# Moving a layer norm's shift and sums to VectorE, holding condition rows behind the norm, and splitting pool bands inside the short convolution

## The chip, the cores and the metric

The kernel runs on one core of a Trainium2 chip. The metric is the device time of one execution in microseconds. In the text PE is TensorE, DVE is VectorE, ACT is ScalarE, POOL is GpSimd and SP is SyncE, whose queue issues the DMAs.

## The reference

One step of a backbone of four layers for 128 context tokens and 256 latent tokens, D = 1024, in float32. Each layer has a mixer and an MLP, each followed by a layer norm of a scaled residual. The mixers are: a gated linear recurrence (layers 0 and 3), a short gated convolution (layer 1), a pooling mixer (layer 2).

```python
for i in range(DEPTH):
    mod = jax.nn.silu(cond) @ p['w_mod'][i] + p['b_mod'][i]
    sh1, sc1, g1, sh2, sc2, g2 = jnp.split(mod[:, None, :], 6, axis=-1)
    h = x * (1 + sc1) + sh1
    ...                                   # out = mixer(h)
    x = layer_norm(ALPHA * x + g1 * out, p['ln_g'][i, 0], p['ln_b'][i, 0])
    h = x * (1 + sc2) + sh2
    f = squared_relu_mlp(h, p['mlp_w1'][i], p['mlp_b1'][i], p['mlp_w2'][i], p['mlp_b2'][i])
    x = layer_norm(ALPHA * x + g2 * f, p['ln_g'][i, 1], p['ln_b'][i, 1])
```

The pooling mixer takes windowed means of 2, 4, 8 and 16 tokens in four groups of channels; the kernel does that as a product with banded matrices.

## The kernel before, in words

**Layout.** Features lie on the 128 partitions, the 384 tokens (128 + 256) along the free axis. The residual stream is eight tiles `X0` to `X7` of 128 x 384, one for each 128 features ("column" c below).

**Products.** A float32 product is done as three matmuls (L198, L199, L200): each weight and each activation is split into a rounded part `hi` and a rest `lo`, and hi x hi, lo x hi and hi x lo are summed in PSUM. One weight tile of 128 x 128 with its three matmuls is called a tile here. Weights come as 1 MB blocks of 16 tiles by DMA (L1275, four buffers `raw`), and a block is split in two halves of 8 tiles: ACT writes `whi` (L1287), DVE writes `wlo` (L1293). The split of a half is asked for three halves ahead of its use.

**Order of work.** The program is a list `items` of blocks in order: `X` (a function), `G` (a function with a loaded block), and halves of weights. Every tile is a tick; `defer(n, fn)` runs `fn` n ticks later. From that the framework makes one fixed queue for each engine: it may move an instruction ahead of earlier ones of the program when its inputs are there. `tc.issue_after(ins)` puts instructions behind `ins` in the queue of its engine, without a semaphore.

**Layer norm.** `ln_evac` runs while the product ahead of the norm is computed. For each finished column c, `resid` (L556, two DVE instructions for the two token groups) adds the gated output to `X[c]`. Once column 0 is there, `shift` takes its mean over the partitions (L578 on PE, L579 on ACT into `ssb`) and subtracts it from all eight columns (L581), which keeps the variance formula well conditioned. `stat` then squares each column (L592, ACT) and adds columns and squares into the running sums `s1t` (L596) and `s2t` (L598). With `fast=True` (the recurrence layers and the pooling layer) the subtractions of columns 3 to 7 and the sums `s2t` are on DVE; the subtractions of columns 0 to 2 and `s1t` are on POOL. With `late=True` (the pooling layer alone) the shift is on DVE already and the squares are summed on PE. In all other norms shift and sums are on POOL.

`ln_tail` follows. `stats_a` sums over the partitions on PE: `s1t` (L620), `s2t` (L622), the last column (L623) and its square (L624). Condition products (`gemv`, L348) fill PE while DVE and ACT do the tail: variance (L652), reciprocal root (L653, ACT), centring (L643), one Newton step (L657 to L659), scaling (L663) and the next `h` (L698, L703, L716, L721, L760). The last instruction of the tail, the `lo` half of `h` of column 7 on DVE, is kept as `hcur["end"]`.

**MLP.** `up` (L819 to L822) makes the hidden tiles `hid`, in `hi` and `lo`; the down projection reads them in order of k, 16 at a time.

**Condition rows.** Some of the modulation vectors are computed on DVE during the MLPs (`mac`, L453): products of weight rows (`fetch`, L445, two buffers in the tile `mac`) with the row `silb`, which is silu of the condition, repeated on all partitions. `silb` is made once, at the start of the first MLP, by `setup_rows`: a tanh (L429, ACT), a scale (L430, DVE) and a product (L431, DVE) over 2048 elements each. It uses the second `mac` buffer as its scratch, so the second `fetch` comes behind it. The products L453 are already held behind `hcur["end"]`.

**Bands.** `band_load(i)`, i = 0 and 1, loads a block of band matrices and splits it (L1091 on ACT, three L1095 on DVE). They are needed by the pooling mixer in layer 2. In the program they stand between the second layer norm and the short convolution of layer 1.

## Time and profile before

| | us |
|---|---|
| median of 3 runs | 1624.18 (1623.5 to 1624.21) |
| the profiled execution | 1623.76 |
| its span | 1621.9 |
| PE busy in it | 1569.9 |
| DVE busy | 1158.7 |
| ACT busy | 750.6 |
| POOL busy | 392.8 |
| granted PE clock, mean | 0.996 |

A row of the profile's timeline gives the start, the duration, the engine, the line of the kernel, the operation, what it writes and reads with the shapes, how many like it were merged, and in brackets the idle time of the engine ahead of it with what ended it. Times are microseconds from the start of the span. Rows of one engine overlap a little, since an instruction may start while the last one drains; the distance from start to start is then shorter than the duration.

### The profile page before, as it was taken

Reading aid. Unit: us, or ns where it says so; the run is one execution under the profiler, and the core shown is the slowest. Engines: PE = TensorE matmul, PEld = TensorE weight load, DVE = VectorE, ACT = ScalarE, POOL = GpSimd, SP = SyncE. Lnnn points to the kernel's source line nnn. Section 1 sums busy time; section 2 is a strip of 40 time slices with the busy share of each in tenths; the row PEclk is TensorE's granted clock in tenths of the full one; section 3 lists DMA queues with packets and bytes.
Section 4 is the critical chain, followed back from the end, with each engine's and each line's share of the span. In section 5 each row is a group of like instructions: output and inputs, shape, how many; then the busy total and the mean of one; then the engine's idle time right before and its main releaser. Section 6 shows DMA issues by size and latency. Waiting matters only on the chain.

```text
span 1621.9 us, 23848 instructions
## 1 busy us (share of the span) xinstructions
PE 1569.9 (97%) x9388; PEld 1500.4 (93%) x9388; DVE 1158.7 (71%) x1786; ACT 750.6 (46%) x1129; POOL 392.8 (24%) x410
## 2 busy tenths in 40 slices
PE   6999899999999999999999999999999989999996
PEld 6778799999989989999998799999988779999996
DVE  4789899974475559994545999974468997434544
ACT  3796553244352336423434653244359947423432
POOL 2113290001430067300043290000431134000043
PEclk9999999999999999999999999999999999999999
DMA  9677457755353345765453357745333444333321
GB/s 361 264 277 275 138 204 256 266 201 208 130 176 115 139 181 194 243 229 181 139 197 131 144 208 255 268 159 197 120 118 104 161 141 154 122 117 125 130 78 39
DMA packets 42591, 289.79 MB, mean 179 GB/s; under 512 B 4848, under 2 KB 7024, under 8 KB 8432
## 3 DMA queue, kind: packets, MB, share of 16 engines
q1 hardware_dynamic: 42480, 288.28, 49.8%
q8 instruction: 73, 1.20, 0.3%
q14 instruction: 38, 0.31, 0.0%
HBM read 286.67 MB, written 1.59 MB: 178 GB/s over the span
## 4 chain that ended last, share of the span: by engine, by line
PE 79%; DVE 12%; ACT 5%; issue 2%; DMA 1%; POOL 1%; SPq 0%; DVEq 0%; POOLq 0%; ACTq 0%
PE acc L199 25%; PE acc L198 25%; PE acc L200 25%; DVE wlo L1293 2%; DVE lru L868 1%; ACT hidf L919 1%; DMA raw<-in_wmod 1%; DVE X L556 1%; DVE hidf L947 1%; DVE hidf L936 1%; ACT L922 1%; ACT hidf L922 1%; DVE X L663 1%; DVE X L581 0%; ACT L932 0%
## 5 line engine op out<-in xcount | busy, mean ns | idle before, releaser
L1287 ACT ACTIVATE whi<-raw 128x1024 fp32r<-128x1024 f32 x338 | 356.1, 1056 | 413.4 <-PE acc L200 345.2
L1293 DVE TENSOR_TENSOR wlo<-raw,whi 128x1024 fp32r<-128x1024 f32 x338 | 435.3, 1289 | 154.9 <-ACT whi L1287 154.4
L198 PE MATMUL acc<-h,whi 128*128 128x384 f32 (+2 forms) x1472 | 499.0, 339 | 7.2 <-DVE h L698 6.7
L199 PE MATMUL acc<-h,wlo 128*128 128x384 f32 (+2 forms) x1472 | 498.3, 339 | 0.0
L200 PE MATMUL acc<-h,whi 128*128 128x384 f32 (+2 forms) x1472 | 468.8, 339 | 0.0
L198 PE MATMUL acc<-hid,whi 128*128 128x384 f32 (+1 forms) x1216 | 411.3, 338 | 0.8 <-ACT hid L964 0.8
L200 PE MATMUL acc<-hid,whi 128*128 128x384 f32 (+1 forms) x1216 | 409.9, 337 | 0.8 <-DVE hid L968 0.8
L199 PE MATMUL acc<-hid,wlo 128*128 128x384 f32 (+1 forms) x1216 | 409.2, 336 | 0.0
L198 PEld LDWEIGHTS acc<-h,whi 128*128 128x128 f32 x1472 | 277.1, 188 | 14.7 <-issue 10.0
L199 PEld LDWEIGHTS acc<-h,wlo 128*128 128x128 f32 x1472 | 277.0, 188 | 1.0 <-issue 0.2
L200 PEld LDWEIGHTS acc<-h,whi 128*128 128x128 f32 x1472 | 273.7, 188 | 1.0 <-DVE X L643 0.4
L198 PEld LDWEIGHTS acc<-hid,whi 128*128 128x128 f32 x1216 | 228.4, 188 | 2.3 <-ACT hid L964 1.4
L200 PEld LDWEIGHTS acc<-hid,whi 128*128 128x128 f32 x1216 | 228.2, 188 | 1.5 <-DVE hid L968 1.5
L199 PEld LDWEIGHTS acc<-hid,wlo 128*128 128x128 f32 x1216 | 228.2, 188 | 0.9
L453 DVE SCALAR_TENSOR_TENSOR mac<-mac,silb 128x1024 f32<-128x1024 f32 x176 | 216.3, 1229 | 1.7
L819 ACT ACTIVATE tmp<-acc,par 128x384 f32<-128x384 f32 x128 | 74.2, 580 | 248.1 <-PE acc L200 248.1
L581 POOL TENSOR_TENSOR X<-X,ssb 128x384 f32<-128x384 f32 x46 | 52.5, 1178 | 488.1 <-ACT ssb L579 488.1
L821 DVE TENSOR_TENSOR tmp<-tmp 128x384 f32<-128x384 f32 x128 | 73.2, 572 | 104.1 <-ACT tmp L819 104.1
L556 DVE SCALAR_TENSOR_TENSOR X<-acc,m,X 128x128 f32<-128x128 f32 (+1 forms) x176 | 64.6, 410 | 109.2 <-PE acc L200 109.2
L771 POOL TENSOR_SCALAR X<-X,ag,xbb 128x128 f32<-128x128 f32 x64 | 134.2, 2112 | 0.4
L822 DVE TENSOR_TENSOR hid<-tmp,hid 128x384 fp32r<-128x384 f32 x128 | 72.2, 564 | 0.3
L596 POOL TENSOR_TENSOR s1t<-s1t,X 128x384 f32<-128x384 f32 x40 | 43.7, 1092 | 114.4 <-DVE X L556 111.1
(192 smaller groups left out, 1192.4 us busy)
## 6 DMA issues: line engine op xcount, KB each, us to landing
raw<-in_w SPq DMA_DIRECT2D x128, 1024.0 KB, 4.9
mac<-in_wmodv SPq DMA_DIRECT2D x44, 1024.0 KB, 5.2
raw<-in_wmodp SPq DMA_DIRECT2D x26, 1024.0 KB, 4.9
park<-in_wmodp SPq DMA_DIRECT2D x18, 1024.0 KB, 8.4
raw<-in_lin SPq DMA_DIRECT2D x16, 1024.0 KB, 4.9
raw<-in_scin SPq DMA_DIRECT2D x12, 1024.0 KB, 4.8
raw<-in_wmod SPq DMA_DIRECT2D x8, 1024.0 KB, 7.7
raw<-in_lout SPq DMA_DIRECT2D x8, 1024.0 KB, 5.0
```

Source lines behind the costliest of these rows:

```text
L198: pe.matmul(ps, lhsT=hi, rhs=xhi, start=first, stop=False)
L199: pe.matmul(ps, lhsT=lo, rhs=xhi, start=False, stop=False)
L200: late = lambda: pe.matmul(ps, lhsT=hi, rhs=xlo, start=False, stop=last)
L453: vec.scalar_tensor_tensor(prod, raw[i % 2][:, D * q : D * q + D], 1.0, silb[:, D * k : D * k + D], op0=ALU.mult, op1=ALU.mult, accum_out= ...
L556: vec.scalar_tensor_tensor(Xt[c][:, o : o + n], ps[:, a:b], col(g, c, k), Xt[c][:, o : o + n], op0=ALU.mult, op1=ALU.add)
L581: (vec if late or fast and i > 2 else gp).tensor_tensor(Xt[i], Xt[i], ssb, op=ALU.subtract)
L771: gp.tensor_scalar(Xt[c][:, a:b], Xt[c][:, a:b], col(g, c, k), col(xb, c, k), op0=ALU.mult, op1=ALU.add)
L819: act.activation(r, ps[:, :T], AF.Relu, bias=par_t[:, i : i + 1])
L821: vec.tensor_tensor(q, r, r, op=ALU.mult)
L822: vec.tensor_tensor(lo, q, hi.bitcast(F32), op=ALU.subtract)
L1287: act.activation(hi, raws[id(raw)][:, i * 1024 : (i + 1) * 1024], AF.Copy)
L1293: vec.tensor_tensor(lo, raws[id(raw)][:, i * 1024 : (i + 1) * 1024], hi.bitcast(F32), op=ALU.subtract)
```

## The change

Three edits. (1) In the norms with `fast=True` and not `late`, which are the first norms of layers 0 and 3, all eight subtractions of the shift and the six additions of `s1t` are issued on DVE. (2) The three instructions of `setup_rows` are issued inside `tc.issue_after(hcur["end"].ins)`. (3) `band_load(0)` and `band_load(1)` are inserted into the short convolution's items, behind its 10th and its 12th half of weights.

```diff
     def setup_rows(t):
         nc.sync.dma_start(silb, crow)
-        defer(6, lambda: act.activation(t, silb, AF.Tanh, scale=0.5))
-        defer(10, lambda: vec.tensor_scalar(t, t, 1.0, 0.5, op0=ALU.add, op1=ALU.mult))
-        defer(14, lambda: vec.tensor_tensor(silb, t, silb, op=ALU.mult))
+
+        def behind(fn):
+            def f():
+                with tc.issue_after(hcur["end"].ins):
+                    fn()
+
+            return f
+
+        defer(6, behind(lambda: act.activation(t, silb, AF.Tanh, scale=0.5)))
+        defer(10, behind(lambda: vec.tensor_scalar(t, t, 1.0, 0.5, op0=ALU.add, op1=ALU.mult)))
+        defer(14, behind(lambda: vec.tensor_tensor(silb, t, silb, op=ALU.mult)))
         rows_ready.append(True)
...
             for i in [0] + held if late else range(C):
-                (vec if late or fast and i > 2 else gp).tensor_tensor(Xt[i], Xt[i], ssb, op=ALU.subtract)
+                (vec if late or fast else gp).tensor_tensor(Xt[i], Xt[i], ssb, op=ALU.subtract)
...
             if 0 < c < 7:
-                gp.tensor_tensor(s1t, Xt[0] if c == 1 else s1t, Xt[c], op=ALU.add)
+                (gp if late else s2eng).tensor_tensor(s1t, Xt[0] if c == 1 else s1t, Xt[c], op=ALU.add)
...
     ln_tail(2, to_h(2, "mm"), use)
-    band_load(0)
-    band_load(1)
+    here = len(items)
     use = short_conv(1)
+    for i in range(2):
+        band_load(i)
+        items.insert(here + 11 + 3 * i, items.pop())
     ln_tail(3, to_h(3, "mm"), use)
```

## The prediction

> **What bounds the kernel now.** I read the page first, then who TensorE (PE) waits for, then each of the three stretches that the diff touches in order of time, engine by engine.

> ```profile
> span 1621.9 us, 23848 instructions
> PE 1569.9 (97%) x9388; PEld 1500.4 (93%) x9388; DVE 1158.7 (71%) x1786; ACT 750.6 (46%) x1129; POOL 392.8 (24%) x410
> ```

> ```profile
> PE acc L620 <- POOL s1t L596: 7.0, 2, 5.1
> ...
> PE acc L198 <- DVE h L698: 6.7, 6, 2.0
> ```

> PE is busy for 1569.9 of 1621.9 us, so only what ends a PE pause can move the end. The second fence lists such pauses (total us, times, longest). The line with POOL's running sum `s1t` stands for exactly two pauses, 5.1 and 1.9 us: the first layer norm of layer 0 ("first site") and of layer 3 ("second site"), where the diff moves work. The third place is the layer norm before the short convolution ("band site"), one of the six pauses before L198.

> First site, rows of PE, DVE, ACT and POOL in order of time (start, us, what, count, idle before):

> ```profile
> 151.85 1.92 ACT L429 ACTIVATE mac<-silb 128x2048 f32<-128x2048 f32 x1 [1.14 <-DVE hid L968]
> 153.68 1.04 ACT L1287 ACTIVATE whi<-raw 128x1024 fp32r<-128x1024 f32 x1
> 153.80 1.23 DVE L430 TENSOR_SCALAR mac<-mac 128x2048 f32<-128x2048 f32 x1 [0.26 <-ACT mac L429]
> ...
> 155.18 4.45 POOL L581 TENSOR_TENSOR X<-X,ssb 128x384 f32<-128x384 f32 x3 [6.41 <-ACT ssb L579]
> 156.08 4.91 DVE L581 TENSOR_TENSOR X<-X,ssb 128x384 f32<-128x384 f32 x5
> ...
> 165.58 2.28 DVE L431 TENSOR_TENSOR silb<-mac,silb 128x2048 f32<-128x2048 f32 x1
> ...
> 169.09 1.28 ACT L602 ACT_TABLE_LOAD   x1
> ...
> 170.00 2.02 DVE L1293 TENSOR_TENSOR wlo<-raw,whi 128x1024 fp32r<-128x1024 f32 x1
> ...
> 173.29 2.26 POOL L596 TENSOR_TENSOR s1t<-s1t,X 128x384 f32<-128x384 f32 x2 [2.35 <-DVE X L556]
> ...
> 175.60 1.65 PE L620 MATMUL acc<-s1t,ones_m 128*128 128x384 f32 x2 [5.11 <-POOL s1t L596]
> 175.89 0.73 DVE L556 SCALAR_TENSOR_TENSOR X<-acc,m,X 128x128 f32<-128x128 f32 x2
> 177.04 1.49 PE L622 MATMUL acc<-s2t,ones_m 128*128 128x384 f32 x2
> ...
> 181.20 0.56 DVE L652 SCALAR_TENSOR_TENSOR tmp<-acc,tmp 128x384 f32<-128x384 f32 x1 [4.58 <-PE acc L624]
> 181.68 1.01 DVE L643 TENSOR_TENSOR X<-X,acc 128x384 f32<-128x384 f32 x2
> 182.60 0.55 DVE L657 TENSOR_TENSOR tmp<-tmp,tmp 128x384 f32<-128x384 f32 x1
> ...
> 183.75 1.90 PE L348 MATMUL acc<-raw,sil 128*32 128x256 f32 x32
> ...
> 185.84 0.41 PE L198 MATMUL acc<-h,whi 128*128 128x384 f32 x1 [0.19 <-DVE h L698]
> ```

> The reader sees three things. PE has finished the mixer's matmuls at 175.60 - 5.11 = 170.49. The last residual (L556 at 175.89) is 5.4 us later than that, because DVE runs behind: L430 and L431, which belong to the next stage, sit in its queue, and its rows are stretched while POOL reads the same tiles: five subtractions take 4.91 beside POOL's three, while two of the same size take 0.92 from start to start (181.68 to 182.60) when POOL is quiet. And the pause also costs afterwards: the two statistics matmuls of L622 last 1.49 here against 0.81 at the second site.

> Second site:

> ```profile
> 1312.76 4.91 DVE L581 TENSOR_TENSOR X<-X,ssb 128x384 f32<-128x384 f32 x5 [0.46 <-ACT ssb L579]
> ...
> 1322.91 1.21 DVE L1293 TENSOR_TENSOR wlo<-raw,whi 128x1024 fp32r<-128x1024 f32 x1
> ...
> 1325.33 2.03 DVE L556 SCALAR_TENSOR_TENSOR X<-acc,m,X 128x128 f32<-128x128 f32 x6
> ...
> 1330.00 0.91 PE L620 MATMUL acc<-s1t,ones_m 128*128 128x384 f32 x2 [1.94 <-POOL s1t L596]
> 1330.29 0.73 DVE L556 SCALAR_TENSOR_TENSOR X<-acc,m,X 128x128 f32<-128x128 f32 x2
> 1330.75 0.81 PE L622 MATMUL acc<-s2t,ones_m 128*128 128x384 f32 x2
> ...
> 1332.96 0.56 DVE L652 SCALAR_TENSOR_TENSOR tmp<-acc,tmp 128x384 f32<-128x384 f32 x1 [1.95 <-PE acc L624]
> ```

> Same picture without the condition rows: PE ends at 1328.06, the last residual at 1330.29 + 0.73 = 1331.0, and `s1t` keeps PE only 1.94 us.

> **The change part by part.**

> *Shifts and sums to DVE.* POOL loses three subtractions and six `s1t` additions at each of the two sites; DVE gets them. Its unstretched step is 0.46 us (above), a pair of residual halves 0.68 (2.03 for six halves), a weight split 1.21. The work between the shift and the last residual is then 8 subtractions + 6 `s1t` + 6 `s2t` = 20 x 0.46 = 9.2, 7 pairs = 4.7, 2 splits = 2.4: 16.3 us in all. At the second site it starts at 1312.76 and ends at 1329.1; PE's own end would allow 1328.06 + 0.1 + 0.7 = 1328.9, so DVE is just about the limit. Gain 1331.0 - 1329.1 = 1.9; the square of the last column and its matmul follow in the same way. I take 1.7, because the ACT table load (1.28) sits in the chain of squares that `s2t` waits for. Bounds: 2.1 (PE's end) and -0.5 (if DVE's steps came to 0.58 each, 20 x 0.12 = 2.4 more).

> *Condition rows behind the first layer norm.* The two DVE instructions L430 and L431 (1.23 + 2.28 = 3.5) leave the first site; ACT's L429 (1.92) ran beside the matmuls and the row after it shows no wait for it, so it may stay or go at no cost here. There the first split can start when its high half is ready, 153.68 + 1.04 = 154.72, ends at 155.9, and the same 16.3 us put the last residual at 172.2 instead of 176.6. PE's floor is 170.49 + 0.8 = 171.3. From there: square 0.5, one statistics pair 0.65 (1330.00 to 1330.75 and on, less its overlap), so L652 starts at about 173.5 instead of 181.20: 7.7 us. Of these 4.4 are the earlier residual, and the rest is that three of the four statistics pairs no longer stand behind the late `s1t` at the slow rate. What follows is unchanged: L652 to the first matmul is 4.64 us (181.20 to 185.84), and PE fills it with the condition matmuls of L348, which end at 185.65. I take 7.3, with 0.4 off for the table load; ends 8.6 (PE's floor) and 3.5 (only the two rows' time comes back).

> *What the moved rows cost later.* They now stand behind the last instruction of the norm, where the next MLP starts:

> ```profile
> 240.00:280.00 40.00, 40.00 (x231) 40.00 (x231) 39.79 (x65) 14.14 (x18) 0.39 (x2) 1.00 0.73 252
> ...
> 253.13 0.34 PE L198 MATMUL acc<-hid,whi 128*128 128x384 f32 x1
> ...
> 257.90 0.56 DVE L822 TENSOR_TENSOR hid<-tmp,hid 128x384 fp32r<-128x384 f32 x1
> ...
> SPq L445 <- DVE silb L431: 11.3, 1, 11.3
> ```

> (The first row is a stretch of the MLP: PE, PE loads, DVE, ACT, POOL busy.) DVE has no room there, 39.79 of 40 us, so 3.5 us stay as a backlog. Behind them on DVE are the weight splits, the hidden-layer halves and the condition products L453, which need the rows. The tightest reader is the down projection: a tile of PE's work is three matmuls, 0.52 us (231 matmuls in 40 us), so its 16th k comes at 253.13 + 15 x 0.52 = 260.9; that low half is ready at 257.90 + 0.56 = 258.5, 2.4 us ahead. A backlog of 3.5 leaves PE 1.1 us short at worst; the low half is used by the third matmul of a tile only (0.35 later), and some of the backlog falls on L453. I take 0.3, ends 0 and 1.1; if the tanh L429 were held back too, with a table load, 1.92 + 1.28 = 3.2 more is the outer end. SP: the second condition load L445 waited 11.3 us for L431 and nothing behind it was late; it now waits for the later L431, with weight loads of the MLP behind it. Each block feeds PE for 16 x 0.52 = 8.3 us, and there are four buffers; I put nothing on it.

> *Band splits into the short convolution.* The band site, then a stretch of the short convolution:

> ```profile
> 454.25 0.59 DVE L1095 TENSOR_TENSOR fine<-raw,band 128x256 fp32r<-128x256 f32 x3 [4.56 <-ACT band L1091]
> ...
> 457.69 0.56 DVE L652 SCALAR_TENSOR_TENSOR tmp<-acc,tmp 128x384 f32<-128x384 f32 x1 [1.87 <-PE acc L624]
> 458.60 1.07 ACT L1091 ACTIVATE band<-raw 128x1040 fp32r<-128x1040 f32 x1 [1.17 <-DMA raw<-in_band]
> 459.58 0.51 ACT L653 ACTIVATE tmp<-tmp 128x384 f32<-128x384 f32 x1
> 460.09 1.91 PE L348 MATMUL acc<-raw,sil 128*32 128x256 f32 x32
> 460.19 0.56 DVE L657 TENSOR_TENSOR tmp<-tmp,tmp 128x384 f32<-128x384 f32 x1 [1.01 <-ACT tmp L653]
> ...
> 463.71 0.41 PE L198 MATMUL acc<-h,whi 128*128 128x384 f32 x1 [1.71 <-DVE h L698]
> ```

> ```profile
> 500.00:515.00 15.00, 15.00 (x88) 15.00 (x87) 8.70 (x16) 4.46 (x6) 0.00 (x0) 1.00 0.42 140
> ```

> ACT's queue stands for the second band's DMA and then splits it (458.60) before the reciprocal root L653, which was ready at 458.25. L652 to the first matmul takes 6.02 here, 4.64 at the first site: 1.4 us too long. PE's condition matmuls end at 462.0, before the new 462.3, so they don't take the gain. The moved work is two ACT splits (1.07 each), six small DVE instructions (0.59 for three) and two DMAs past 10 and 12 half blocks of SP's weight loads. It lands some 42 and 50 us after 463.71 (a half block is 8 tiles, 4.2 us), where DVE has 6 and ACT 10 of 15 us free. The loads keep a lead of three half blocks. Cost 0, gain 1.4; ends 1.7 (the whole pause) and 0.

> *The sum.* 7.3 + 1.7 + 1.4 - 0.3 = 10.1 us. The profiled execution took 1623.76, 0.4 below the median of the runs (1624.18): 1623.76 - 10.1 = 1613.7. The sum with all ends kind is 8.6 + 2.1 + 1.7 = 12.4, which gives 1611.4.

> [...] PE's slow statistics follow a pause of 5.11 us, those after 1.94 are fast; what lies between these two the trace does not show, and 3 pairs x 0.65 = 2.0 us hang on it. [...]

> **The rivals.**

> (a) *DVE becomes the late engine at the first site.* If its queue puts splits or waits for squares ahead of the `s1t` additions, the sums come 3 us or more after PE's end and the slow rate stays. The DVE row of 16.3 us leaves no idle at all, which speaks for it; that the last column's eight tiles (8 x 0.52) give DVE 4.2 us from about 166.3 on, in which PE brings it nothing new, speaks against. Then 2.0 for the slow pairs and 1 of delay are lost: about 1616.7.

> (b) *The backlog stops PE in the MLP.* With L429 held back as well the backlog is 6.7 us, 4.3 beyond the 2.4 of margin, of which 0.3 is in the sum: 1613.7 + 4.0 = 1617.7. ACT's free time speaks against, DVE's full row for it.

> (c) *The rows are not moved:* an order among DVE's instructions alone, or a schedule that keeps L430 in the norm. The first site then gains about 4.2: 1616.8.

> (d) *Slower:* the long DVE rows are DVE's own and not POOL's doing. At 0.93 a step (as in the stretched 4.91 for five) nine more instructions cost 8.4 us at the second site and 8.4 - 3.5 at the first; with -1.4 for the bands about 1634. It decides from a step of roughly 0.75 on; the 0.46 of L643 without POOL speaks strongly against.

> **How the numbers follow.** Forecast, all three parts as summed (1611.4 to 1615.5): 0.70. (a) 0.12, (b) 0.07, (c) 0.05, (d) 0.02, and 0.04 for gains eaten elsewhere, near no change. The time predicted is the first one's, 1613.7. The range reaches from the kind ends, 1611.4, past (a), (b) and (c) to 1618.5. What a measurement here can tell from no change is about 0.2%, 3.2 us; faster by more than that: 0.94, within 0.03, slower 0.03.

> **What will show it.** In the changed profile L581 and L596 at both sites are DVE rows of some 0.5 us each, and POOL is quiet there; the wait of L620 on POOL is gone, with less than 1.5 us in its place; L622 at the first site takes 0.81; L430 and L431 lie after the norm's last `h`; L653 at the band site follows L652 at once and the wait there is about 0.3. The forecast is wrong if L620 waits for DVE for over 3 us, if PE waits for `hid` L822 or a split at the start of the down projection, or if DVE's steps stay near 0.9 without POOL.

## The result, and the profile after

The changed kernel takes 1616.08 us (median of 4 runs, 1615.73 to 1617.12) against 1624.2 (4 runs, 1623.5 to 1625.98): a ratio of 0.9947, 95% interval 0.9935 to 0.996. A later set of more runs gave 1616.25 (5 runs) against 1625.6 (12 runs), 0.9946 (0.9933 to 0.9958). The prediction said 1613.7, between 1611.4 and 1618.5. The profiled execution took 1615.74, 8.02 less than the one before.

In the changed kernel the lines from about L436 on stand 8 lower in the file: L429 to L431 are L437 to L439, L556 is L564, L581 is L589, L596 is L604, L620 to L624 are L628 to L632, L652 is L660, L698 is L706. Behind the moved bands it is 10: L1287 is L1297, L1293 is L1303. In the variants below the numbers shift again; there the names of the tiles say which row it is.

The page's first part and the table of PE's waits, after:

```profile
span 1614.0 us, 23830 instructions
PE 1567.8 (97%) x9388; PEld 1499.6 (93%) x9388; DVE 1155.0 (72%) x1804; ACT 750.7 (47%) x1129; POOL 373.7 (23%) x392
```

```profile
PE acc L198 <- DVE h L706: 5.5, 6, 2.0
...
PE acc L628 <- DVE s1t L604: 2.0, 2, 1.0
```

The two pauses behind `s1t` went from 7.0 us to 2.0, and it is now DVE that ends them. The waits ahead of L198 went from 6.7 to 5.5.

The first site after (rows of ACT, DVE and PE in the timeline; POOL has none between 150 and 190 us):

```profile
152.93 1.92 ACT L437 ACTIVATE mac<-silb 128x2048 f32<-128x2048 f32 x1 [1.14 <-DVE hid L976]
...
155.82 1.23 DVE L1303 TENSOR_TENSOR wlo<-raw,whi 128x1024 fp32r<-128x1024 f32 x1 [1.20 <-ACT whi L1297]
156.97 3.83 DVE L589 TENSOR_TENSOR X<-X,ssb 128x384 f32<-128x384 f32 x8
...
171.87 0.55 DVE L604 TENSOR_TENSOR s1t<-s1t,X 128x384 f32<-128x384 f32 x1
172.34 0.55 DVE L606 TENSOR_TENSOR s2t<-s2t,tmp 128x384 f32<-128x384 f32 x1
172.81 0.48 DVE L564 SCALAR_TENSOR_TENSOR X<-acc,m,X 128x256 f32<-128x256 f32 x1
175.50 0.56 DVE L660 SCALAR_TENSOR_TENSOR tmp<-acc,tmp 128x384 f32<-128x384 f32 x1 [2.22 <-PE acc L632]
...
195.06 1.22 DVE L438 TENSOR_SCALAR mac<-mac 128x2048 f32<-128x2048 f32 x1
```

```profile
172.57 0.88 PE L628 MATMUL acc<-s1t,ones_m 128*128 128x384 f32 x2 [1.00 <-DVE s1t L604]
173.29 0.81 PE L630 MATMUL acc<-s2t,ones_m 128*128 128x384 f32 x2
173.93 0.81 PE L631 MATMUL acc<-X,ones_m 128*128 128x384 f32 x2
174.58 0.81 PE L632 MATMUL acc<-tmp,ones_m 128*128 128x384 f32 x2
...
180.14 0.41 PE L198 MATMUL acc<-h,whi 128*128 128x384 f32 x1 [0.30 <-DVE h L706]
```

Eight subtractions now take 3.83 us, 0.47 each from start to start; five took 4.91 beside POOL. The pause is 1.00 us, the statistics matmuls run at 0.65 a pair, and L438, the first moved row on DVE, stands behind the norm. The tanh on ACT (L437) did not move, although its line is wrapped in the same way: it still runs ahead of the norm, at 152.93 (L429 at 151.85 before). The second site after, and the end of PE's work at the band site:

```profile
1321.15 0.35 DVE L564 SCALAR_TENSOR_TENSOR X<-acc,m,X 128x128 f32<-128x128 f32 x1 [0.35 <-PE acc L200]
1321.41 0.55 DVE L604 TENSOR_TENSOR s1t<-s1t,X 128x384 f32<-128x384 f32 x1
1321.88 0.55 DVE L606 TENSOR_TENSOR s2t<-s2t,tmp 128x384 f32<-128x384 f32 x1
1322.11 0.88 PE L628 MATMUL acc<-s1t,ones_m 128*128 128x384 f32 x2 [1.00 <-DVE s1t L604]
1322.35 0.48 DVE L564 SCALAR_TENSOR_TENSOR X<-acc,m,X 128x256 f32<-128x256 f32 x1
1325.04 0.56 DVE L660 SCALAR_TENSOR_TENSOR tmp<-acc,tmp 128x384 f32<-128x384 f32 x1 [2.22 <-PE acc L632]
```

```profile
451.98 0.56 DVE L660 SCALAR_TENSOR_TENSOR tmp<-acc,tmp 128x384 f32<-128x384 f32 x1 [1.87 <-PE acc L632]
...
456.70 0.41 PE L198 MATMUL acc<-h,whi 128*128 128x384 f32 x1 [0.40 <-DVE h L706]
```

From the variance row to the first matmul the band site now takes 4.72 us, not 6.02. The two band splits on ACT stand at 479.72 and 489.21, 23 and 33 us behind that matmul, and between 457 and 520 us no row of PE shows a wait.

To see where time goes in any variant I cut each trace at two kinds of rows that all of them have, the start of the shift (`ssb`, L579 or its counterpart) and of the variance (L652 or its counterpart), eight norms each. Where nothing was changed, the traces agree to some 0.1 us between these points, so what differs can be put to a place. Three things are outside that: the slow stretches of experiment 4, the band column of the four traces with unmoved bands, which spreads over 0.4 (112.98 to 113.38), and the start, which spreads over 1 us even without a slow stretch. The columns: start of the first shift; first site, shift to variance; second norm's variance to third norm's shift (it holds the band site); fifth variance to sixth shift (unchanged code); second site, shift to variance; start of the last variance row. The variants are explained below.

| trace | start | first site | band | 5th to 6th | second site | last |
|---|---|---|---|---|---|---|
| before | 154.62 | 26.58 | 113.24 | 217.66 | 20.73 | 1609.76 |
| before, second | 155.36 | 26.59 | 112.98 | 217.64 | 20.74 | 1610.32 |
| after | 155.69 | 19.81 | 111.92 | 217.67 | 19.76 | 1601.82 |
| after, second | 156.39 | 19.80 | 111.92 | 217.64 | 19.77 | 1602.53 |
| after, third | 154.93 | 19.80 | 111.92 | 219.20 | 19.77 | 1602.58 |
| sums alone | 154.91 | 19.97 | 113.38 | 217.64 | 19.79 | 1602.71 |
| rows alone | 155.54 | 22.83 | 113.09 | 217.66 | 20.73 | 1606.84 |
| bands alone | 155.11 | 26.59 | 111.91 | 219.17 | 22.24 | 1612.37 |
| column 6 on PE | 155.40 | 19.86 | 111.91 | 219.19 | 19.82 | 1603.19 |
| its square on PE | 155.59 | 19.54 | 111.91 | 219.19 | 19.17 | 1602.36 |
| idle POOL adds | 154.65 | 26.73 | 111.92 | 219.20 | 25.91 | 1615.36 |
| pauses filled | 155.30 | 19.80 | 111.92 | 217.65 | 19.76 | 1601.76 |
| square and two fills | 155.53 | 19.54 | 111.92 | 217.64 | 19.19 | 1600.76 |

Between the first two traces (before and after): 6.77 won at the first site, 1.32 at the band site, 0.97 at the second site, 1.07 lost before the first shift, in code that the change does not touch; 7.94 in all (with 0.05 lost between, by differences of a few hundredths).

### The profile page after: what moved, and what is told of

Same layout as the page of the kernel before. It is cut to its first block, busy times and chain, and to the rows that moved or that the text cites. A ratio compares the mean times of both kernels' runs of the same rounds, so it can differ in the third digit from the quotient of the medians.

```text
span 1614.0 us, 23830 instructions
## 1 busy us (share of the span) xinstructions
PE 1567.8 (97%) x9388; PEld 1499.6 (93%) x9388; DVE 1155.0 (72%) x1804; ACT 750.7 (47%) x1129; POOL 373.7 (23%) x392
## 4 chain that ended last, share of the span: by engine, by line
PE 81%; DVE 11%; ACT 5%; issue 1%; DMA 1%; POOL 0%; SPq 0%; DVEq 0%; POOLq 0%; ACTq 0%
PE acc L199 26%; PE acc L200 26%; PE acc L198 26%; DVE wlo L1303 2%; DVE lru L876 1%; ACT hidf L927 1%; DMA raw<-in_wmod 1%; DVE hidf L955 1%; DVE X L564 1%; DVE hidf L944 1%; ACT L930 1%; ACT hidf L930 1%; DVE X L671 1%; ACT L940 0%; DVE hidf L952 0%
## 5 line engine op out<-in xcount | busy, mean ns | idle before, releaser
L1297 ACT ACTIVATE whi<-raw 128x1024 fp32r<-128x1024 f32 x338 | 356.1, 1056 | 413.7 <-PE acc L200 345.5
L1303 DVE TENSOR_TENSOR wlo<-raw,whi 128x1024 fp32r<-128x1024 f32 x338 | 433.4, 1283 | 155.0 <-ACT whi L1297 154.7
L198 PE MATMUL acc<-h,whi 128*128 128x384 f32 (+2 forms) x1472 | 498.5, 339 | 6.0 <-DVE h L706 5.5
L198 PE MATMUL acc<-hid,whi 128*128 128x384 f32 (+1 forms) x1216 | 411.2, 338 | 0.8 <-ACT hid L972 0.8
L198 PEld LDWEIGHTS acc<-h,whi 128*128 128x128 f32 x1472 | 276.8, 188 | 13.5 <-issue 8.2
L198 PEld LDWEIGHTS acc<-hid,whi 128*128 128x128 f32 x1216 | 228.4, 188 | 2.3 <-ACT hid L972 1.4
L589 POOL TENSOR_TENSOR X<-X,ssb 128x384 f32<-128x384 f32 x40 | 44.1, 1139 | 467.5 <-ACT ssb L587 467.5
L564 DVE SCALAR_TENSOR_TENSOR X<-acc,m,X 128x128 f32<-128x128 f32 (+1 forms) x176 | 65.4, 412 | 114.9 <-PE acc L200 114.9
L600 ACT ACTIVATE tmp<-X 128x384 f32<-128x384 f32 x64 | 33.0, 517 | 75.9 <-DVE X L564 61.4
```

The costliest lines, as they stand in the source:

```text
L198: pe.matmul(ps, lhsT=hi, rhs=xhi, start=first, stop=False)
L564: vec.scalar_tensor_tensor(Xt[c][:, o : o + n], ps[:, a:b], col(g, c, k), Xt[c][:, o : o + n], op0=ALU.mult, op1=ALU.add)
L589: (vec if late or fast else gp).tensor_tensor(Xt[i], Xt[i], ssb, op=ALU.subtract)
L1297: act.activation(hi, raws[id(raw)][:, i * 1024 : (i + 1) * 1024], AF.Copy)
L1303: vec.tensor_tensor(lo, raws[id(raw)][:, i * 1024 : (i + 1) * 1024], hi.bitcast(F32), op=ALU.subtract)
```

## The experiments

**1. Each edit alone.** The sums alone:

```diff
-                (vec if late or fast and i > 2 else gp).tensor_tensor(Xt[i], Xt[i], ssb, op=ALU.subtract)
+                (vec if late or fast else gp).tensor_tensor(Xt[i], Xt[i], ssb, op=ALU.subtract)
...
-                gp.tensor_tensor(s1t, Xt[0] if c == 1 else s1t, Xt[c], op=ALU.add)
+                (gp if late else s2eng).tensor_tensor(s1t, Xt[0] if c == 1 else s1t, Xt[c], op=ALU.add)
```

> Only the shift and the `s1t` sums on DVE; the condition rows and the bands stay as before. My theory (POOL stretches DVE's rows, and the rows' 2.2 us of L431 stay in the queue): the last residual of the first site comes 2 us earlier than before, L620's wait is 3 to 3.5 us, gain 4.4 there if PE's clock stays up and 2 if it falls; second site 1.0; in all 3 to 5.4 us faster. Rival (the moved condition rows are the gain, the move off POOL only adds nine steps to DVE): no gain at either site, or a loss of some us.

The rows alone (`setup_rows` of the change, the rest as before):

> Only the condition rows held behind the norm; shift, sums and bands as before. My theory: `s1t` on POOL ends about 2.2 us earlier, L620 waits some 2.9 us instead of 5.1, the statistics pairs run at 0.65 each again: gain 5 at the first site, 2.4 if the clock still falls; nothing elsewhere. Rival (POOL's sums set the end whatever DVE does): under 1 us. If the parts were independent, a, b and c would add up to the whole change's 8.1; by my theory a + b is more than the whole gains at the first site (6.8), because both remove the same slow statistics.

The bands alone:

```diff
-    band_load(0)
-    band_load(1)
+    here = len(items)
     use = short_conv(1)
+    for i in range(2):
+        band_load(i)
+        items.insert(here + 11 + 3 * i, items.pop())
```

> Only the band splits moved. My theory: L653 no longer stands behind the band split, the wait of L198 there falls from 1.7 to 0.4: 1.3 us faster, and no new wait in the short convolution. Rival (the splits only move the delay): no change.

Measured, against 1625.9 (18 runs, 1623.96 to 1629.27): sums alone 1617.55, ratio 0.9952 (0.994 to 0.9965); rows alone 1620.99, 0.9969 (0.9959 to 0.998); bands alone 1626.63, 1.0002 (0.9993 to 1.0011).

The sums alone were worth 8.35 us, more than the 3 to 5.4 that I expected; the rows alone 4.91, near the 5. By the table, the sums alone win 6.61 of the 6.77 at the first site, the rows alone 3.75. They are two cures of one lateness and do not add: tying the rows is worth 0.16 once the sums are on DVE. Why, the DVE rows with the sums alone say:

```profile
154.10 1.23 DVE L430 TENSOR_SCALAR mac<-mac 128x2048 f32<-128x2048 f32 x1 [0.25 <-ACT mac L429]
155.24 1.22 DVE L1293 TENSOR_TENSOR wlo<-raw,whi 128x1024 fp32r<-128x1024 f32 x1
...
172.18 0.48 DVE L556 SCALAR_TENSOR_TENSOR X<-acc,m,X 128x256 f32<-128x256 f32 x1
172.57 2.28 DVE L431 TENSOR_TENSOR silb<-mac,silb 128x2048 f32<-128x2048 f32 x1
174.88 0.56 DVE L652 SCALAR_TENSOR_TENSOR tmp<-acc,tmp 128x384 f32<-128x384 f32 x1
```

In this kernel's queue of DVE L431 stands behind the last residual, in the time in which DVE waits for the statistics; it ends at 174.85, and the variance starts at 174.88, 0.93 behind the start of PE's last statistics pair (173.95), as in the changed kernel (174.58 and 175.50). So L431 costs nothing there. Only L430 still stands ahead.

With the rows alone POOL still works beside DVE, and PE's rows are:

```profile
174.04 0.91 PE L628 MATMUL acc<-s1t,ones_m 128*128 128x384 f32 x2 [2.63 <-POOL s1t L604]
174.79 0.91 PE L630 MATMUL acc<-s2t,ones_m 128*128 128x384 f32 x2
175.49 1.49 PE L631 MATMUL acc<-X,ones_m 128*128 128x384 f32 x2
176.77 1.49 PE L632 MATMUL acc<-tmp,ones_m 128*128 128x384 f32 x2
```

A pause of only 2.63 us, and the slow rate still came, for two of the four pairs. These two cost 1.3 us more than at 0.65 each (1.28 from 175.49 to 176.77), which is what the rows alone lack at the site, 3.75 where 5 was expected.

The bands alone do in their own stretch what they do in the whole change (111.91), and yet the time shows nothing of the 1.3 us that I expected: two stretches of unchanged code, fifth to sixth and second site, took 1.5 us more each in the one trace there is. What the other ten runs lost no trace shows. Its second site, where the pause is the one of before:

```profile
1331.09 0.91 PE L620 MATMUL acc<-s1t,ones_m 128*128 128x384 f32 x2 [1.90 <-POOL s1t L596]
1331.84 1.06 PE L622 MATMUL acc<-s2t,ones_m 128*128 128x384 f32 x2
1332.69 1.49 PE L623 MATMUL acc<-X,ones_m 128*128 128x384 f32 x2
```

After a pause of 1.94 the same matmuls took 0.81 in the first trace. The edit does not touch these matmuls; experiments 4 and 5 go after it.

**2. What sets the end of the sites now.** Column 6 and its square are left out of DVE's sums and given to PE as two matmuls of their own (the diff shows the issue; L604 and L606 are skipped for c = 6):

```diff
+            if c == 6 and fast and not late:
+                hcur["sq6"] = sq[6]
...
+                pe.matmul(m1[:, :T], lhsT=ones_m, rhs=Xt[6], start=False, stop=False)
+                pe.matmul(m2[:, :T], lhsT=ones_m, rhs=sq6, start=False, stop=False)
```

> The changed kernel, and at the two sites column 6 and its square are no longer added into `s1t` and `s2t` on DVE but summed on PE with two more matmul pairs, as column 7 is. In the changed kernel PE waits 1.0 us for the last `s1t` and then runs four pairs of 0.65 behind each other. My theory: that queue behind the last sum is what the prediction missed; with two DVE steps less and the first four pairs done before the last residual, L652 comes 1.5 to 1.8 us earlier at each site, about 3.3 us below the changed kernel, so some 11.4 below before. Rival (DVE's whole work up to the last residual is the limit, the order of the pairs does not matter): only the two steps, 0.9 per site, less 0 to 1.3 for the two pairs more, so -0.4 to +0.9 per site.

1617.04, ratio 0.9947 (0.9934 to 0.9959), no better than the change, where I had expected 3.3 us less, and the sites take 19.86 and 19.82. The pause is gone, as expected, and six pairs stand where four stood:

```profile
171.11 0.81 PE L630 MATMUL acc<-s1t,ones_m 128*128 128x384 f32 x2
...
174.33 0.81 PE L638 MATMUL acc<-tmp,ones_m 128*128 128x384 f32 x2
```

Two more pairs cost 1.3 us, the pause was 1.0. So I gave PE the square alone, summed right behind `s2t`, ahead of `s1t`:

> The changed kernel with the square of column 6 left out of DVE's sum at the two sites and given to PE as a matmul of its own (0.65 us). With column 6 and its square on PE (the run before) the stop behind s1t was gone, but six statistics matmuls of 0.65 in a row took what was gained: the reciprocal root's input came 19.86 us after the shift, as in the changed kernel (19.81). Theory 'PE's row of statistics matmuls sets the end': five of them, starting as soon as PE is free, give about 19.2 at both sites, 1.2 us in all, 0.07% of the time. Rival 'DVE sets it': 19.8, no change.

The sites take 19.54 and 19.17: 0.27 and 0.59 won, 0.86 of the 1.2 that I expected. At the first site PE's second pair, the square of column 6, starts 0.85 us behind the first (172.16 and 171.31), 0.2 more than the 0.65 of the others. The median does not show 0.9 us: 1616.32 against 1616.25 for the change, ratio 0.9944 (0.9932 to 0.9957); this trace had a slow stretch from 912 us on.

**3. Is the stretch of DVE's rows POOL's doing?**

```diff
+            if 0 < c < 7 and fast and not late:
+                gp.tensor_tensor(dum, Xt[c], ssb, op=ALU.add)
```

> The changed kernel with one idle addition on POOL per column 1 to 6 at both sites (X[c] + ssb into a tile nobody reads). Theory 'POOL beside DVE stretches both': DVE's steps of 0.47 that run beside one of POOL's six additions go to about 0.93; six additions of some 1.1 us each cost DVE about 2.8 us per site, the stop of PE behind s1t grows from 1.0 to 3 or more, and the kernel takes 4 to 8 us longer than the changed one. Rival 'the long rows were DVE's own': the DVE steps stay as they are and the time too.

1629.17 (7 runs), ratio to before 1.0026 (1.0015 to 1.0037): 12.9 us over the change, more than the 4 to 8 that I expected, and slower than before. DVE and POOL at the first site:

```profile
168.53 1.86 POOL L605 TENSOR_TENSOR dum<-X,ssb 128x384 f32<-128x384 f32 x1 [0.96 <-DVE X L565]
169.43 1.37 DVE L607 TENSOR_TENSOR s1t<-s1t,X 128x384 f32<-128x384 f32 x1
170.73 0.55 DVE L609 TENSOR_TENSOR s2t<-s2t,tmp 128x384 f32<-128x384 f32 x1
...
176.01 1.62 PE L631 MATMUL acc<-s1t,ones_m 128*128 128x384 f32 x2 [5.49 <-DVE s1t L607]
```

An addition beside a POOL addition takes 1.37, the next one, beside nothing, 0.55. The 0.82 us more is near the time of one POOL addition (0.99 for the shortest of `s1t` in the trace of before), and the DVE row ends 0.41 us behind the POOL row (170.80 and 170.39), as if it had waited for that one to end; the cause of it the rows do not show. The long rows were not DVE's own: one idle POOL instruction per column gives back the whole gain of the first site (26.73) and at the second costs 5.2 more than before (25.91 against 20.73), part of it by the slow statistics (1.62 and 1.49 for the first two pairs) behind a pause of 4.78. I had the stretch too small, 0.8 per instruction and not 0.46, and had left out that the pause, 5.49 again, brings the slow statistics (1.62) back.

**4. The slow stretches in unchanged code.** Start of the recurrence's gate matmuls in the first trace of before and of after:

```profile
64.02 2.85 PE L882 MATMUL acc<-lru,raw 128*128 128x388 f32 x8 [1.84 <-DVE lru L868]
```

```profile
63.62 4.54 PE L890 MATMUL acc<-lru,raw 128*128 128x388 f32 x8 [1.84 <-DVE lru L876]
```

The same pause, the same work, 1.7 us more. The trace of after was 0.4 ahead at this point, so it is 1.3 behind after it, and 1.07 of that is left at the first shift. More traces of the unaltered kernels:

> The changed kernel once more, unaltered. In the first trace of it one block of the first recurrence (eight gate matmuls x2) took 4.54 us against 2.85 before, at a granted clock of 0.5, after a pause of 1.84 us that both kernels have. Theory 'chance': such falls, each some 3.4 us long and worth about 1.5 us, come after pauses of about 2 us in code that the change does not touch, now here, now there; this run shows them at another place or not at all, and everything between the falls takes the same time as in the first trace to 0.1 us. Rival 'the change slows the start': the same block is slow again, at 64 us, in this trace too.

> The kernel before once more, unaltered, for a second trace at another phase of the window. Theory 'free-running window': the falls in it start a whole number of 3.413 us apart; a fall after the pauses at 64, 919 and 1330 us is there exactly where one window of that grid holds more than about 1.85 us of idle time, and each of them makes its stretch 1.5 us longer. Rival 'each kernel has its falls at fixed places': the same as in the first trace of it, the first site alone. At the first site the slow statistics (1.49) are there in both.

> The changed kernel a third time. Both traces of it so far had a fall at 64 us, and no trace of any other kernel had. Theory 'free-running window': its start on the grid is by chance, so that the fall at 64 us is there or not according to the idle time of the window, and one may stand at 912 us instead. Rival 'the change causes the fall at 64 us': it is there again whatever the grid says.

The second trace of the changed kernel had the slow block at 64 us again, against my theory so far. The third did not, and had a slow stretch at 912 us instead (rows of its windows: length, busy times of PE, PE loads, DVE, ACT, POOL, then granted clock, DMA share and GB/s):

```profile
64.00:68.00 4.00, 3.67 (x14) 2.62 (x15) 3.25 (x5) 2.71 (x6) 0.00 (x0) 1.00 1.00 414
...
912.00:916.00 4.00, 4.00 (x25) 2.29 (x25) 4.00 (x9) 3.94 (x9) 0.00 (x0) 0.57 1.01 428
```

So the place is not fixed by the kernel. Cutting the clock column finely in all traces, every slow stretch (a granted clock of 0.50) up to the last norm lasts 3.41 us or twice that, and their starts within one trace lie whole multiples of 3.4133 us apart: 63.99 - 16.20 = 14 of them in the first trace after, 919.25 - 175.15 = 218 and 1332.26 - 919.25 = 121 with the bands alone, 888.76 - 175.38 = 209 with the rows alone. Against the start of the span the grid lies anywhere: 0.38, 0.66, 0.85, 1.45 and 2.55 us past a whole multiple of 3.4133 in five of the traces. Those that cost time in the table (1.5 us each: the fifth-to-sixth column at 219.2, the second site at 22.24 with the bands alone) come just behind a pause of 1.9 to 2.0 us. The one at 888.76 with the rows alone costs nothing there; the window of the grid ahead of it holds two shorter pauses, 1.28 and 0.52 us. Counted over the 11 traces that have both pauses unfilled, 64 us was hit twice, both times in the changed kernel, and 912 us five times.

My rule for which pauses are hit fell: I expected a slow stretch exactly where one window of the grid holds over 1.85 us of idle time. In the second trace of before the second site's pause puts 1.91 us into one window and nothing follows; with the bands alone 1.90 was enough. The place of the pause on the grid, which my rule left out, does sort the hits. The pause of 1.97 at 912 us was followed by a slow stretch in exactly the five traces in which it begins 0.24 to 1.14 us behind the start of a window, and not in the six in which it begins at 1.41 or later; in one of these, the rows alone, all 1.97 lie in one window too. The pause of 1.84 at 64 us lies in one window in all eleven traces; it was followed by one in exactly the two in which it begins at 1.20 and 1.23, and not in the nine in which it begins at 0.14 to 0.73. So the place on the grid accounts for the two hits of the changed kernel, without the edit. Idle time alone does not decide; why these places count, and not the same ones at both pauses, stays open.

**5. Filling the pauses.** Unread matmuls of constants in PE's longest pauses:

```diff
+    def fill(n):
+        if n:
+            d = acc()
+            for i in range(n):
+                pe.matmul(d[:, :P], lhsT=ones_m, rhs=ones_m, start=True, stop=True)
```

> The changed kernel with 19 matmuls of constants (128 columns each) whose result nobody reads, in PE's longest pauses: 4 in the 1.84 us pause of the first recurrence, 3 and 3 in two pauses (1.5, 1.7) of the second, 4, 3 and 2 behind the condition matmuls of three layer norms (pauses 1.97, 1.27, 1.16). Theory 'chance clock falls after pauses of about 2 us': the pauses get shorter than 1 us, no fall is seen in the trace at these places, the median is 0.5 to 2 us under that of the changed kernel and the runs lie closer together. Rival 'the pauses do not matter': falls as before and the time the same; and if the extra matmuls reach past their pauses, up to 1 us more.

No slow stretch at the filled places, but none of the 0.5 to 2 us that I expected: 1616.21 (1615.68 to 1616.38), ratio 0.9944 (0.9931 to 0.9956). The stretch that holds the fills of the second recurrence, sixth variance to seventh shift, takes 120.25 us for 119.90. The fills do not reach past their pauses, since PE still waits 0.86 and 1.12 us behind them; PE waits longer later on, 1.40 us for 0.59, for ACT's `hid`. Why, and where the rest of the expected gain went, is not shown. Then only the two pauses that had been hit, with the square of column 6 on PE:

> The changed kernel with the square of column 6 on PE (as in the run that gave 0.27 us at the first and 0.6 at the second site), and four unread matmuls of constants in each of the two pauses that have been followed by a clock fall in some traces and not in others: 1.84 us in the first recurrence (64 us) and 1.97 us in the norm before the third MLP (912 us). The falls seen so far last 3.41 us or twice that, each, and begin at multiples of 3.413 us from each other within a trace. Theory 'a free-running window of 3.41 us with over about 1.8 us idle in it halves the clock for the next one': with less than 1 us left of each pause no fall can come at either place, whatever the phase; no fall is in the trace between 25 and 1600 us apart from one near 890 that costs nothing; the median comes to 1614 to 1615.4. Rival 'falls come regardless of the length of the pause': falls at 64 or 912 as before and a median of 1616.

1614.61 (1614.05 to 1615.92), inside the 1614 to 1615.4 that I expected, ratio 0.9933 (0.9919 to 0.9946); its trace shows no slow stretch before the last norm. By chance it has the same phase of the grid as the trace with the square alone (the last norm's slow stretch starts at 1605.72 and 1605.71), and 912 us comes at the same time, so the two can be laid side by side, although they ran on two chips. Each with a row or two of PE's timeline and a window; square alone first, then square and fills:

```profile
911.60 0.41 PE L198 MATMUL acc<-h,whi 128*128 128x384 f32 x1 [1.97 <-DVE h L712]
```

```profile
912.00:916.00 4.00, 4.00 (x26) 2.29 (x25) 4.00 (x9) 3.92 (x8) 0.00 (x0) 0.60 1.01 428
```

```profile
909.53 1.16 PE L572 MATMUL acc<-ones_m 128*128 128x128 f32 x8
911.57 0.41 PE L198 MATMUL acc<-h,whi 128*128 128x384 f32 x1 [0.88 <-DVE h L719]
```

```profile
912.00:916.00 4.00, 4.00 (x34) 3.17 (x34) 4.00 (x9) 3.94 (x8) 0.00 (x0) 1.00 1.01 424
```

The first matmul starts within 0.03 us of the same moment, and only the kernel without the fill loses its clock (217.64 against 219.19 in the table). This is the best version here, 1.6 us under the change's median, which was taken on another chip (1616.25, with before at 1625.6 there and at 1625.93 here); the two intervals of the ratio overlap. 0.84 of it is seen at the two sites. The rest, 0.8, is about half of one slow stretch, and the eleven unfilled traces show seven at the two filled places; that the rest comes from there is argued, not shown, since filling alone won nothing.

## Why the prediction was right, and where its sizes were off

| term | predicted | first two traces |
|---|---|---|
| first site | -7.3 | -6.77 |
| second site | -1.7 | -0.97 |
| band site | -1.4 | -1.32 |
| backlog in the MLP | +0.3 | 0.00 |
| code not touched | 0 | +1.07 |

The profile carries the forecast's parts better than the median does: 1616.08 lies inside the whole range, but outside the 1611.4 to 1615.5 of the case that I gave 0.70, and close to what rivals (a) and (c) would have given (1616.7 and 1616.8). That it was not one of these is shown by the rows, not by the number.

**First site.** The last residual ends 17.60 us after the shift (172.81 + 0.48 - 155.69); the prediction put it at 172.2 - 154.62 = 17.58. What failed is the step behind it, from the last residual to the variance, "square 0.5, one statistics pair 0.65": it takes 2.21. The step "three of the four statistics pairs no longer stand behind the late `s1t`" was wrong. All four do: `s1t` at 171.87 is still the thing that PE waits for, and four pairs of 0.65 follow in a row. The 0.4 that had been taken off for the table load covered part, 0.5 is missing. In PE's terms the gain is 4.1 of pause (5.11 to 1.00) and 2.7 of statistics at full rate (L620 to L652 took 5.60, now 2.93).

The attribution was wrong too, though not the sum: the moved rows were credited with their 3.5 us, and are worth 0.16 behind the sums. Rival (c), 1616.8 if the rows stayed, falls with that: with the rows unmoved the first site lost 0.16, not 3.1.

**Second site.** 0.73 short. The residual's last half ends at 1322.83, 1.72 us after PE's end (1322.11 - 1.00), where the prediction allowed 0.1 + 0.7 and put DVE's own end 0.2 later. The rows above show why: PE gives DVE the first part of the last column at 1321.15, and `s1t` and `s2t` of column 6 (0.94) stand between that and the last half. Another 0.27 is lost behind the residual: from its end to the variance it took 1.94 before and takes 2.21 now, where the prediction had it unchanged. Giving that square to PE won 0.59.

**Bands and backlog.** The wait at the band site is 0.40, where 0.3 was predicted. The splits landed earlier than the 42 and 50 us that I had worked out, 23 and 33, and cost nothing there. The backlog cost nothing: from the first norm's variance to the second norm's shift, which is the first MLP, it takes 216.33 us in before, with the sums alone and in the changed kernel. The hidden half that the sum feared for was in time:

```profile
251.95 0.55 DVE L830 TENSOR_TENSOR hid<-tmp,hid 128x384 fp32r<-128x384 f32 x1
```

```profile
SPq L453 <- DVE silb L439: 4.7, 1, 4.7
```

SP's wait for the rows even fell from 11.3 to 4.7, with nothing behind it late. Rival (a) is out by the pause of 1.00. Rival (b) was not put to the test as stated, since the tanh was not held back (L437 at 152.93); the smaller backlog did not stop PE. Rival (d) is out by 0.47 a step and by experiment 3; its own terms, 8.4 + 4.9 - 1.4 on 1623.76, add up to 1635.7 and not to 1634.

**Untouched code.** The remaining 1.07 is the slow block at 64 us. Without it, in the third trace, the changed kernel reaches the first shift at 154.93; in all traces without a slow block there the start lies between 154.62 and 155.59, in whichever kernel. So it belongs to the pause, which before has too, and to its place on the grid, not to the change; without it the sum of the first two traces is 9.0 us, and the medians of the larger set of runs differ by 9.35 (1625.6 - 1616.25).

**The clock after a pause.** The sum counts every statistics pair at full rate, 0.65. Up to which length a pause costs only itself, no run shows: pauses of 1.84, 1.90, 1.97 and 2.63 us were followed by the slow rate, and others of 1.84, 1.94 and 1.97 by the full one. The sites stayed clear of this: in the changed kernel the pause there is 1.00 us, and the pairs behind it run at 0.64 to 0.72 from start to start.

## What to carry to other kernels

Two edits that cure the same lateness must not be added up: ask of the second what is still late when the first is in, and look for an instruction that already stands in a wait for another engine once the first is in. Follow the end of a stage to its last reader: here a row of four short matmuls still stood behind one late sum. When a trace shows a loss in code that was not changed, cut several traces at the same rows; a loss that moves from place to place is not the edit's, and small gains are read in their own stretch, not in the total.
